# A one-core decoder trunk: how the first arrays are loaded, three filler matmuls, and two places in attention's order

## The chip, the core and the metric

The kernel runs on one core of a Trainium2 chip. The metric is the device time of one execution in microseconds (us); smaller is better. TensorE does the matmuls (PE in the rows, PEld where it loads weights), ScalarE is ACT, VectorE is DVE, GpSimd is POOL, and SyncE is SP, which here only starts transfers. ACT and POOL can start transfers too. A transfer started by any of them is carried out by the core's 16 DMA engines.

## The reference

The input is one sequence of 256 positions with 1024 features in float32. There are two layers. The first is an mLSTM mixer followed by a convolutional feed-forward network; after it, keys and values are computed once from the residual stream. The second is block-sparse attention over those keys and values (with one block of 256 it is plain causal attention), followed by a second feed-forward network. Cut to what matters here:

```
def mlstm_mixer(x, norm_g, w_in, b_gates, h_norm_g, w_out):
    u = rmsnorm(x, norm_g) @ w_in
    q, k, v, o, gi, gf = jnp.split(u, M_SPLITS, axis=-1)
    ...
    h = mlstm_chunkwise(q, k, v, i_pre, f_pre)
    ...
    return h.astype(x.dtype) @ w_out

def shared_kv(x, norm_g, w_kv, k_norm_g, cos, sin):
    kv = rmsnorm(x, norm_g) @ w_kv
    ...

for l in range(DEPTH):
    if l < N_A:
        h = h + mlstm_mixer(...)
    else:
        h = h + moba_mixer(...)
    h = h + conv_ffn(...)
    if l == N_A - 1:
        kb, vb, kmean = shared_kv(h, kv_norm, w_kv, k_norm, cos, sin)
```

## The kernel before

**Tiling.** The residual stream is held transposed in `hT`, eight tiles of 128 features by 256 positions, k = 0 to 7. Every float32 operand is split into a high and a low part in the format float32r, and each product is made of three: high by high, high by low, low by high. ACT makes the high part and DVE the low part (lines 155 to 171). Weights come in units of up to 128 x 2048 elements (1 MB) through three raw buffers and four high/low pairs.

**The start.** Lines 123 to 135 start the first transfers: `hT` in five pieces, the small array `fst` (the gate weights and the first norm's gains, 36 KB), the first weight unit `raw0` in four pieces of 512 columns, and the second unit `raw1` in two. Each column block of 256 in `raw0` belongs to one k. The first two pieces of `raw0` are started by ACT, all else by SP. Every transfer from SP and ACT counts its landing in one of eight semaphores in turn, and waits, before it starts, for the earlier transfer that used the same one.

`warm_up` (lines 146 to 151) gives TensorE ten matmuls on zeros (fillers) while the data come. Then lines 408 to 415 write out by hand, for ACT and DVE, the order in which `hT` is scaled and split into `xa` (which needs `fst`) and `raw0` is split: for k = 0 and 1 each `xa` tile and its weight block, afterwards two `xa` tiles and then a double block of weights. Lines 554 to 557 are the matmuls: for each k two products of two matmuls each (lines 241 and 245) and one for the gates (line 548), k after k; after k = 0 two more fillers stand.

**Attention.** `mix` (line 70) lays small pieces of other work between the matmul steps of a projection; each piece has a due time in estimated us, and it goes in ahead of the first step that begins at or after it. `block_x` is sixteen steps of three matmuls (lines 262 to 264), eight for each half t of the positions; after the eighth step of a half its result goes to `done`. On lines 815 to 828 these pieces are: `r.sums` (the sum of squares over features, line 212, which needs `sqacc` and gives `rc` by way of DVE and POOL; `heads` needs `rc`), `turn` (transposes of query or key heads, line 753, copied out by ACT at line 754), `turn_p` (three transposes of a head's weights, line 781, split by line 168/169 and copied by line 783), `logits` and `values`. `turn` and `turn_p` take their PSUM bank from one set of three (`mis`), so each waits until an earlier one's bank has been read out.

TensorE's order is the program's order everywhere. The order on ACT, DVE and POOL is written by hand up to line 593 for ACT and DVE, and made by the language's scheduler elsewhere.

Of the kernel before, what the change touches and what calls it, by code (L numbers as in the profile page):

```python
# [21 lines left out]
KD = D // P  # L22
# [14 lines left out]
AHEAD = 2  # L37
GROUP = 4
HOLD = 4
WARM = 10  # L40
FILL = 2
WHOLE = 6
PIECES = 2

# [25 lines left out]
def mix(steps, items=()):  # L70

    items, now = list(items), 0.0
    for cost, step in steps:
        while items and items[0][0] <= now:
            items.pop(0)[1]()
        step()
        now += cost
    for _, item in items:
        item()
# [3 lines left out]
def yoco_kernel(ctx: ExitStack, tc: tile.TileContext, A, out):  # L83
    nc = tc.nc
# [30 lines left out]
    hT = keep.tile([P, KD, S], F32, name="hT")  # L115
    fst = const.tile([P, N_FIRST], F32, name="fst")
# [3 lines left out]
    rope = const.tile([P, NT, 2, ROT], F32, name="rope")  # L120
    raw0 = wraw.tile([P, 2048], F32, name="raw")

    nc.sync.dma_start(hT[:, 0], A["xT"][:, 0])
    nc.sync.dma_start(fst, A["first"])
    nc.sync.dma_start(hT[:, 1], A["xT"][:, 1])
    for j in range(3):
        k = slice(2 * j + 2, 2 * j + 4)
        nc.sync.dma_start(hT[:, k], A["xT"][:, k])
    for j in range(4):
        c = slice(j * 512, (j + 1) * 512)  # L130
        (nc.scalar if j < 2 else nc.sync).dma_start(raw0[:, c], A["w_kq"][0, :, c])
    raw1 = wraw.tile([P, 2048], F32, name="raw")
    for j in range(2):
        c = slice(j * 1024, (j + 1) * 1024)
# [11 lines left out]
    def warm_up(n):  # L146
        for j in range(n):
            ps = bank("acc")
            nc.tensor.matmul(ps, warm[:, :P], warm, start=True, stop=True)

    warm_up(WARM)
    nc.vector.memset(wgs.bitcast(F32), 0.0)


    def unit(src, length, pieces=PIECES):
        raw = wraw.tile([P, 2048], F32, name="raw")[:, :length]
        nc.sync.dma_start(raw, src)
        hi = wsp.tile([P, 2048], F32R, name="hi")[:, :length]
        lo = wsp.tile([P, 2048], F32R, name="lo")[:, :length]
        for j in range(pieces):  # L160
            c = slice(j * length // pieces, (j + 1) * length // pieces)
            nc.scalar.activation(hi[:, c], raw[:, c], AF.Copy)  # L162
            nc.vector.tensor_tensor(lo[:, c], raw[:, c], hi[:, c].bitcast(F32), OP.subtract)  # L163
        return hi, lo
# [20 lines left out]
    def operand(pool, name, n):  # L185
        ts = [pool.tile([P, 2 * S], F32R, name=f"{name}{k}") for k in range(n)]
        return [t[:, :S] for t in ts], [t[:, S:] for t in ts], ts

    setA = operand(keep, "xa", KD)
# [63 lines left out]
    def steps_x(t, units, x, done):  # L253

        xh, xl, _ = x
        ts = slice(t * P, (t + 1) * P)
        ps = Once(acc)

        def one(k):
            (hi, lo), p = units[k // 4](), ps()  # L260
            c = slice((k % 4) * 512, (k % 4 + 1) * 512)
            nc.tensor.matmul(p, xh[k][:, ts], hi[:, c], start=k == 0, stop=False)  # L262
            nc.tensor.matmul(p, xh[k][:, ts], lo[:, c], start=False, stop=False)  # L263
            nc.tensor.matmul(p, xl[k][:, ts], hi[:, c], start=False, stop=k == KD - 1)  # L264
            if k == KD - 1:
                done(t, p)

        return [(0.64, lambda k=k: one(k)) for k in range(KD)]

    def block_x(src, first, x, done, u=None):  # L270

        u = u or [Once(lambda j=j: unit(src[first + j], 2048)) for j in range(2)]
        return [s for t in range(NT) for s in steps_x(t, u, x, done)]
# [125 lines left out]
    first = ExitStack()  # L399
# [55 lines left out]
    with tc.tile_pool(name="mls", bufs=1, reuse_waits="tile") as mp, \  # L455
            tc.tile_pool(name="mlw", bufs=2, reuse_waits="tile") as mw, lend("mlp", "mis"):
        r = Rstd()
# [81 lines left out]
        def kq_steps(j):  # L539
            return steps_w(pk[j], wk[j // 2], lambda k: k * 256 + (j % 2) * P, setA, range(KD), KD,  # L540
                           lambda p: whole(p, kq[j]))
# [12 lines left out]
        for k in range(KD):  # L554
            mix((s0[k], s1[k], sg[k]))
            if k == 0:
                warm_up(FILL)
        mix(kq_steps(2)[:1])
# [143 lines left out]
    with tc.tile_pool(name="att", bufs=1, reuse_waits="tile") as mp, \  # L702
            tc.tile_pool(name="atw", bufs=2, reuse_waits="tile") as mw, lend("atl", "mis"), ExitStack() as st:
        r = Rstd()
# [106 lines left out]
        def it(t, fn, *a):  # L811
            return (t, lambda: fn(*a))

        W = A["w_kqv"]
        mix(block_x(W, 0, setA, heads(0, 0)), [it(4.4, r.sums)])
        mix(block_x(W, 2, setA, heads(0, 1)), [it(3.5, turn, 0, 0, 0), it(8.5, turn, 0, 0, 1)])
        mix(block_x(W, 4, setB, heads(1, 0)), [it(3.5, turn, 0, 1, 0), it(8.5, turn, 0, 1, 1), it(9.2, turn, 1, 0, 0)])
        mix(block_x(W, 6, setB, heads(1, 1)),
            [it(4.5, turn, 1, 0, 1)] + [it(6.0 + 1.2 * h, logits, h) for h in range(4)])
        mix(block_x(W, 8, setA, v_done(0)),  # L820
            [it(0.5, turn, 1, 1, 0), it(1.2, turn_p, 0), it(2.6, turn_p, 1), it(4.8, turn_p, 2),
             it(5.2, turn, 1, 1, 1), it(5.8, turn_p, 3)] + [it(6.2 + 1.2 * h, logits, 4 + h) for h in range(4)])
        early.close()
        pp = st.enter_context(tc.tile_pool(name="atp", bufs=1, reuse_waits="tile"))
        pS += [[pp.tile([P, S], F32R, name=f"p{nm}{h}") for nm in "hl"] for h in range(AH // 2, AH)]
# [75 lines left out]
```

## Time and profile before

| what | value |
|---|---|
| median of 3 runs | 594.1 us (593.5 to 594.26) |
| profiled execution, its own time | 594.04 us |
| span of its trace | 592.3 us |
| time outside the span | 1.74 us |
| TensorE busy in the span | 585.9 us (99%) |
| DVE, ACT, POOL busy | 495.0, 394.7, 161.0 us |

The profile is one execution. Its span begins with the first instruction and ends with the last; 594.04 - 592.3 = 1.74 us lie around it. A busy share says how long an engine had an instruction in work, and the chain of waits says what each stretch of time waited for.

### The profile page before, as it was taken

How to read it: one execution, taken by the hardware profiler on the slowest of the kernel's cores; microseconds unless marked ns; L12 is line 12 of the kernel's file. 1: busy time of each engine (PE TensorE's matmuls, PEld its weight loads, DVE VectorE, ACT ScalarE, POOL GpSimd, SP SyncE). 2: the span in 40 equal slices, each digit the busy share in tenths (PEclk: the TensorE clock that was granted, in tenths of full speed). 3: DMA queues.
4: the chain of work that ended last, by engine and by line, in shares of the span. 5: the costliest groups of instructions: out<-in, count | busy, mean ns of one | idle time of the engine just before them, and what ended most of it. 6: DMA issues, size and time to landing. Idle time of an engine off the chain costs nothing.

```text
span 592.3 us, 9008 instructions
## 1 busy us (share of the span) xinstructions
PE 585.9 (99%) x3266; PEld 503.2 (85%) x3266; DVE 495.0 (84%) x843; ACT 394.7 (67%) x731; POOL 161.0 (27%) x178
## 2 busy tenths in 40 slices
PE   8999999999999999999999999999999999999997
PEld 4888888888888888888888878888888888888887
DVE  6888677799999999988867787577999999998750
ACT  6777776487777767765656687646877867675530
POOL 3001300452445443301221210024335543432000
PEclk9999999999999999999999999999999999999999
DMA  8667334347454533487745533343564455345930
GB/s 284 237 222 274 143 142 146 141 152 275 155 188 160 209 132 135 153 266 240 258 167 214 196 127 134 125 139 133 181 237 151 144 211 188 123 148 191 285 116 19
DMA packets 18621, 105.79 MB, mean 179 GB/s; under 512 B 2320, under 2 KB 3856, under 8 KB 9104
## 3 DMA queue, kind: packets, MB, share of 16 engines
q1 hardware_dynamic: 18288, 104.68, 50.4%
q10 hardware_dynamic: 288, 0.52, 0.3%
q8 instruction: 26, 0.43, 0.3%
q14 instruction: 19, 0.16, 0.1%
HBM read 104.15 MB, written 1.05 MB: 178 GB/s over the span
## 4 chain that ended last, share of the span: by engine, by line
PE 97%; DMA 2%; ACT 0%; DVE 0%; issue 0%
PE acc L241 48%; PE acc L245 25%; PE acc L262 6%; PE acc L264 6%; PE acc L263 6%; DMA raw<-w_kq 2%; PE acc L239 1%; PE mis L635 1%; PE mis L753 1%; PE acc L763 1%; PE mis L807 0%; PE mis L781 0%; PE acc L762 0%; PE mis L808 0%; PE mis L667 0%; PE mis L602 0%
## 5 line engine op out<-in xcount | busy, mean ns | idle before, releaser
L163 DVE TENSOR_TENSOR lo<-raw,hi 128x1024 fp32r<-128x1024 f32 (+1 forms) x210 | 238.4, 1166 | 23.2 <-ACT hi L162 23.0
L241 PE MATMUL acc<-xb,hi 128*128 128x512 f32 x736 | 252.1, 396 | 0.0
L162 ACT ACTIVATE hi<-raw 128x1024 fp32r<-128x1024 f32 (+1 forms) x210 | 193.1, 968 | 41.1 <-PE acc L241 14.9
L245 PE MATMUL acc<-xb,lo 128*128 128x256 f32 x736 | 191.2, 279 | 0.0
L241 PEld LDWEIGHTS acc<-xb,hi 128*128 128x128 f32 x736 | 131.8, 188 | 25.1 <-DVE xb L171 0.2
L245 PEld LDWEIGHTS acc<-xb,lo 128*128 128x128 f32 x736 | 138.7, 188 | 8.0
L241 PE MATMUL acc<-f,hi 128*128 128x512 f32 x330 | 115.0, 393 | 0.0
L330 DVE SCALAR_TENSOR_TENSOR y<-whole,par,y 128x255 f32<-128x255 f32 (+1 forms) x176 | 108.1, 635 | 3.7 <-ACT y L327 3.4
L245 PE MATMUL acc<-f,lo 128*128 128x256 f32 x352 | 96.8, 282 | 0.0
L339 POOL TENSOR_TENSOR a<-sg,y 128x256 f32<-128x256 f32 x44 | 54.3, 1235 | 104.3 <-ACT sg L337 104.2
L241 PEld LDWEIGHTS acc<-f,hi 128*128 128x128 f32 x330 | 61.1, 188 | 13.0
L327 ACT ACTIVATE y<-whole,par 128x256 f32<-128x256 f32 x88 | 52.1, 594 | 25.5 <-DVE whole L283 21.9
L245 PEld LDWEIGHTS acc<-f,lo 128*128 128x128 f32 x352 | 66.1, 188 | 1.3
L241 PE MATMUL acc<-xa,hi 128*128 128x512 f32 x160 | 56.4, 396 | 0.4 <-DVE xa L171 0.4
L341 POOL TENSOR_TENSOR f<-a,f 128x256 fp32r<-128x256 f32 x44 | 43.6, 991 | 39.5 <-ACT f L340 39.5
L262 PE MATMUL acc<-hi,xa 128*128 128x512 f32 x128 | 52.6, 411 | 0.0
L264 PE MATMUL acc<-hi,xa 128*128 128x512 f32 x128 | 50.1, 392 | 0.0
L263 PE MATMUL acc<-lo,xa 128*128 128x512 f32 x128 | 50.0, 390 | 0.0
L199 POOL TENSOR_TENSOR sqacc<-sqacc,sq 128x256 f32<-128x256 f32 x18 | 16.1, 892 | 106.3 <-ACT sq L198 106.2
L245 PE MATMUL acc<-xa,lo 128*128 128x256 f32 x160 | 43.5, 285 | 1.2 <-DVE lo L169 1.2
L283 DVE TENSOR_TENSOR whole<-acc,whole 128x256 f32<-128x256 f32 x89 | 36.2, 412 | 0.0
L282 ACT ACTIVATE whole<-acc 128x256 f32<-128x256 f32 x89 | 32.3, 368 | 5.2 <-DVE y L330 5.2
(193 smaller groups left out, 652.5 us busy)
## 6 DMA issues: line engine op xcount, KB each, us to landing
raw<-w_up SPq DMA_DIRECT2D x44, 1024.0 KB, 4.8
raw<-w_down SPq DMA_DIRECT2D x32, 704.0 KB, 5.0
raw<-w_kqv SPq DMA_DIRECT2D x12, 1024.0 KB, 4.9
raw<-w_vo SPq DMA_DIRECT2D x8, 1024.0 KB, 5.1
raw<-w_out SPq DMA_DIRECT2D x4, 1024.0 KB, 4.8
raw<-w_o SPq DMA_DIRECT2D x4, 1024.0 KB, 4.9
raw<-w_kq SPq DMA_DIRECT2D x2, 1024.0 KB, 8.0
raw<-w_kq SPq DMA_DIRECT2D x2, 512.0 KB, 7.5
```

The costliest lines, as they stand in the source:

```text
L162: nc.scalar.activation(hi[:, c], raw[:, c], AF.Copy)
L163: nc.vector.tensor_tensor(lo[:, c], raw[:, c], hi[:, c].bitcast(F32), OP.subtract)
L241: nc.tensor.matmul(p, hi[:, c], both[k], start=k == 0, stop=last)
L245: nc.tensor.matmul(p[:, :S], lo[:, c], xh[k], start=False, stop=False)
L262: nc.tensor.matmul(p, xh[k][:, ts], hi[:, c], start=k == 0, stop=False)
L263: nc.tensor.matmul(p, xh[k][:, ts], lo[:, c], start=False, stop=False)
L264: nc.tensor.matmul(p, xl[k][:, ts], hi[:, c], start=False, stop=k == KD - 1)
L283: nc.vector.tensor_tensor(y, ps[:, :S], y, OP.add)
L327: nc.scalar.activation(y, u, AF.Identity, bias=b, scale=w[2])
L330: nc.vector.scalar_tensor_tensor(y[:, d:], u[:, :S - d], w[j], y[:, d:], op0=OP.mult, op1=OP.add)
L339: nc.gpsimd.tensor_tensor(out=a, in0=sg, in1=y[0], op=OP.mult)
L341: nc.gpsimd.tensor_tensor(out=al[i], in0=a, in1=ah[i].bitcast(F32), op=OP.subtract)
```

## The change

At the start, `fst` is started by POOL and no longer by SP; `hT` comes in four pieces (k = 0, 1, 2 to 3, 4 to 7); `raw0` comes in three pieces (512, 512 and 1024 columns), all started by ACT. The fillers ahead of the first product go from ten to nine, and the two after k = 0 go. In attention `r.sums` stands behind the eighth step of the first half, just ahead of `heads`, where it stood ahead of the eighth step; and `turn(1, 1, 1)` and `turn_p(2)` change places.

```
-WARM = 10
-FILL = 2
+WARM = 9
+FILL = 0
...
+    nc.gpsimd.dma_start(fst, A["first"])
     nc.sync.dma_start(hT[:, 0], A["xT"][:, 0])
-    nc.sync.dma_start(fst, A["first"])
     nc.sync.dma_start(hT[:, 1], A["xT"][:, 1])
-    for j in range(3):
-        k = slice(2 * j + 2, 2 * j + 4)
-        nc.sync.dma_start(hT[:, k], A["xT"][:, k])
-    for j in range(4):
-        c = slice(j * 512, (j + 1) * 512)
-        (nc.scalar if j < 2 else nc.sync).dma_start(raw0[:, c], A["w_kq"][0, :, c])
+    for k0, k1 in ((2, 4), (4, KD)):
+        nc.sync.dma_start(hT[:, k0:k1], A["xT"][:, k0:k1])
+    for k0, k1 in ((0, 2), (2, 4), (4, KD)):
+        c = slice(k0 * 256, k1 * 256)
+        nc.scalar.dma_start(raw0[:, c], A["w_kq"][0, :, c])
...
-        mix(block_x(W, 0, setA, heads(0, 0)), [it(4.4, r.sums)])
+        def first_done(t, ps):
+            if t == 0:
+                r.sums()
+            heads(0, 0)(t, ps)
+
+        mix(block_x(W, 0, setA, first_done))
...
-            [it(0.5, turn, 1, 1, 0), it(1.2, turn_p, 0), it(2.6, turn_p, 1), it(4.8, turn_p, 2),
-             it(5.2, turn, 1, 1, 1), it(5.8, turn_p, 3)] + [it(6.2 + 1.2 * h, logits, 4 + h) for h in range(4)])
+            [it(0.5, turn, 1, 1, 0), it(1.2, turn_p, 0), it(2.6, turn_p, 1), it(4.6, turn, 1, 1, 1),
+             it(5.2, turn_p, 2), it(5.8, turn_p, 3)] + [it(6.2 + 1.2 * h, logits, 4 + h) for h in range(4)])
```

SP's first transfers before (`xT` goes to `hT`; `w_kq` to `raw0` with 512 columns, to `raw1` with 1024, to the third unit with 2048; DMAHW0 to DMAHW7 are the eight semaphores):

```order
L123 DMA hT<-xT 128x256
L124 DMA fst<-first 128x72
L125 DMA hT<-xT 128x256
L128 DMA hT<-xT 128x512 x3
L131 DMA raw<-w_kq 128x512 [waits DMAHW0_49]
L131 DMA raw<-w_kq 128x512 [waits DMAHW1_49]
L135 DMA raw<-w_kq 128x1024 [waits DMAHW2_49]
L135 DMA raw<-w_kq 128x1024 [waits DMAHW3_49]
L157 DMA raw<-w_kq 128x2048 [waits DMAHW4_49]
```

and in the changed kernel:

```order
L124 DMA hT<-xT 128x256
L125 DMA hT<-xT 128x256
L127 DMA hT<-xT 128x512
L127 DMA hT<-xT 128x1024
L134 DMA raw<-w_kq 128x1024
L134 DMA raw<-w_kq 128x1024 [waits DMAHW0_49]
L156 DMA raw<-w_kq 128x2048 [waits DMAHW1_49]
```

`fst` and the second half of `raw0` have left this queue, and the first half of `raw1` no longer waits for a semaphore.

TensorE in attention before, from the last step of the first half on (`pr` is a head's weights in `turn_p`, `y` the queries in `turn`):

```order
L264 MATMUL acc<-hi,xa_132 128x512
L781 MATMUL mis<-ident,pr_3260 128x128 [waits DVE_49,Activation_49]
L781 MATMUL mis<-ident,pr_3260 128x128 [waits DVE_49]
L781 MATMUL mis<-ident,pr_3260 128x128
L262 MATMUL acc<-hi,xa_125 128x512
L263 MATMUL acc<-lo,xa_125 128x512
L264 MATMUL acc<-hi,xa_125 128x512
L753 MATMUL mis<-ident,y_3743 128x128 [waits Activation_49]
```

and in the changed kernel:

```order
L263 MATMUL acc<-hi,xa_128 128x512
L752 MATMUL mis<-ident,y_3735 128x128 [waits DVE_49,Activation_49]
L752 MATMUL mis<-ident,y_3735 128x128 x3
L261 MATMUL acc<-hi,xa_121 128x512
L262 MATMUL acc<-lo,xa_121 128x512
L263 MATMUL acc<-hi,xa_121 128x512
L780 MATMUL mis<-ident,pr_3252 128x128 [waits Activation_49]
```

The query transposes now come first, and the weight transposes stand where the wait for ACT was.

ACT at the same place before (`pr_3258` is the copy that frees the bank of `turn_p(0)`; `vh` is the first half's result):

```order
L170 ACTIVATE vh<-acc,rc 128x512 [waits PE_49]
L168 ACTIVATE xb_139<-mis 128x256 [waits PE_49]
L783 ACTIVATE pr_3258<-mis 128x128 [waits DVE_49]
L783 ACTIVATE pr_3259<-mis 128x128 [waits DVE_49]
L754 ACTIVATE qT<-mis,gcol 128x4x128 [waits PE_49]
```

and in the changed kernel:

```order
L169 ACTIVATE vh<-acc,rc 128x512 [waits PE_49]
L753 ACTIVATE qT<-mis,gcol 128x4x128 [waits PE_49]
L782 ACTIVATE pr_3250<-mis 128x128 [waits DVE_49]
L782 ACTIVATE pr_3251<-mis 128x128 [waits DVE_49]
L167 ACTIVATE xb_135<-mis 128x256 [waits PE_49]
```

Between `vh` and the copy that frees the bank, the query copy of 128 x 512 now stands in place of a split of 128 x 256.

On POOL the transfer of `fst` stands ahead of all the constants, and the clears now come ahead of all the selects and casts, which were mixed before. Elsewhere two neighbours change places on DVE in attention; nothing else moves.

## Rows read from the trace of the kernel before

**Rows 1.** The page: the span, and the busy time of each engine (share of the span, instructions).

```profile
span 592.3 us, 9008 instructions
PE 585.9 (99%) x3266; PEld 503.2 (85%) x3266; DVE 495.0 (84%) x843; ACT 394.7 (67%) x731; POOL 161.0 (27%) x178
```

**Rows 2.** What TensorE waited for in the whole span: total us, times, longest.

```profile
PE acc L149 <- DVE warm L143: 1.2, 1, 1.2
PE acc L245 <- DVE lo L169: 1.2, 2, 1.0
PE acc L241 <- DVE xa L171: 0.4, 1, 0.4
PE mis L753 <- ACT pr L783: 0.2, 1, 0.2
```

**Rows 3.** The chain that ended last, in order of time, its start: start us, us, what.

```profile
0.80 3.36 DMA raw<-w_kq
4.17 6.85 DMA raw<-w_kq
...
12.46 0.38 PE acc L245
```

**Rows 4.** The timeline of the first 20 us: start us, us, engine, line, what it does, and in brackets the idle time before it and what ended that.

```profile
1.25 4.45 PE L149 MATMUL acc<-warm 128*128 128x512 bf16 x10 [1.25 <-DVE warm L143]
4.43 0.51 ACT L170 ACTIVATE xa<-hT,fst 128x256 fp32r<-128x256 f32 x1 [1.22 <-DMA fst<-first]
4.97 0.95 DVE L171 SCALAR_TENSOR_TENSOR xa<-hT,fst,xa 128x256 fp32r<-128x256 f32 x1 [2.70 <-ACT xa L170]
5.70 0.47 POOL L451 CAST amask<-amaskf 128x256 bf16<-128x256 f32 x1
6.07 0.52 PE L241 MATMUL acc<-xa,hi 128*128 128x512 f32 x1 [0.37 <-DVE xa L171]
6.99 0.48 DVE L171 SCALAR_TENSOR_TENSOR xa<-hT,fst,xa 128x256 fp32r<-128x256 f32 x1 [0.40 <-ACT xa L170]
7.17 0.89 ACT L170 ACTIVATE xa<-hT,fst 128x256 fp32r<-128x256 f32 x2
7.33 0.61 PE L149 MATMUL acc<-warm 128*128 128x512 bf16 x2
9.36 0.39 PE L245 MATMUL acc<-xa,lo 128*128 128x256 f32 x1 [0.30 <-DVE lo L169]
10.18 0.40 PE L548 MATMUL acc<-xa,hi 128*128 128x512 f32 x1
11.11 0.40 PE L548 MATMUL acc<-xa,hi 128*128 128x512 f32 x1
```

**Rows 5.** Transfers, asked for one short stretch at a time: those started at 1.23 us (`fst`), 1.70 (k = 1), 3.08 (k = 6 and 7) and 4.17 (the third piece of `raw0`): from and to, queue, KB, us from the start to the landing.

```profile
fst<-first SPq DMA_DIRECT2D x1, 36.0 KB, 3.1
hT<-xT SPq DMA_DIRECT2D x1, 128.0 KB, 4.7
hT<-xT SPq DMA_DIRECT2D x1, 256.0 KB, 5.1
raw<-w_kq SPq DMA_DIRECT2D x1, 256.0 KB, 6.9
```

**Rows 6.** The first 10 us by stretches: busy time of PE, PEld, DVE, ACT, POOL with counts, then the granted clock, the DMA engines' busy share and GB/s.

```profile
0.00:3.00 3.00, 1.75 (x5) 0.64 (x6) 1.18 (x2) 1.28 (x1) 2.35 (x13) 1.00 0.27 82
3.00:6.00 3.00, 2.70 (x7) 0.67 (x5) 1.03 (x2) 1.17 (x4) 3.00 (x16) 1.00 0.94 231
6.00:9.00 3.00, 2.94 (x12) 1.68 (x12) 2.59 (x7) 2.56 (x7) 0.17 (x1) 1.00 0.99 349
9.00:10.00 1.00, 0.70 (x5) 0.59 (x5) 1.00 (x3) 0.38 (x1) 0.00 (x0) 1.00 1.00 332
```

**Rows 7.** The timeline around two places where the sums of line 212 go between two matmuls: the first layer's (24.45 to 25.36 us) and attention's (301.32 to 302.64).

```profile
24.45 0.40 PE L241 MATMUL acc<-xa,hi 128*128 128x512 f32 x1
25.36 0.40 PE L245 MATMUL acc<-xa,lo 128*128 128x256 f32 x2
...
301.32 0.42 DVE L199 TENSOR_TENSOR sqacc<-sqacc,sq 128x256 f32<-128x256 f32 x1
301.46 0.39 PE L264 MATMUL acc<-hi,xa 128*128 128x512 f32 x1
302.64 0.40 PE L263 MATMUL acc<-lo,xa 128*128 128x512 f32 x1
```

**Rows 8.** The timeline of attention's values block: two transposes of queries and two of weights on TensorE, and ACT between them.

```profile
347.84 0.60 PE L753 MATMUL mis<-ident,y 128*128 128x128 f32 x4
348.97 0.49 PE L781 MATMUL mis<-ident,pr 128*128 128x128 f32 x3
353.80 0.49 PE L781 MATMUL mis<-ident,pr 128*128 128x128 f32 x3
354.00 0.69 ACT L170 ACTIVATE vh<-acc,rc 128x512 fp32r<-128x512 f32 x1 [0.44 <-PE acc L264]
354.59 0.37 ACT L168 ACTIVATE xb<-mis 128x256 fp32r<-128x256 f32 x1
354.85 0.47 ACT L783 ACTIVATE pr<-mis 128x128 f32<-128x128 f32 x2
355.18 0.66 PE L753 MATMUL mis<-ident,y 128*128 128x128 f32 x4 [0.19 <-ACT pr L783]
```

## The prediction

> **What bounds the kernel now.** I read the page's head first: TensorE has an instruction in work for 585.9 of 592.3 us [rows 1]. A busy share does not say that TensorE runs without holes, so the second view is what it waited for: five waits in the whole span, four of them in the first 13 us and one of 0.2 us in attention [rows 2]. So the kernel runs at TensorE's pace from about 13 us on, and an edit is worth what it takes out of those few waits or adds to them. The third view is the chain of waits at the start: it is two transfers of the first weight unit, the second started at 4.17 us, until k = 4 begins on TensorE at 12.46 us [rows 3]. The fourth, the timeline, gives the steps: the first product at 6.07 us, k = 2 at 9.36, and 0.93 us for the five matmuls of one k (from 10.18 to 11.11) [rows 4]. After k = 3 TensorE stands still until 12.46.
>
> **The change part by part.** The profiled execution took 594.04 us, its span and 1.74 us around it, and lies 0.06 us under the median of 594.1; the sum is made against 594.04.
>
> *Loads: when k = 4 can begin.* Two things set it in the changed kernel, and the later one counts.
>
> The first is the data. k = 4 now needs all of `hT` (k = 4 to 7 is one piece) and all of `raw0` (its last 1024 columns are one piece), with `fst` 2084 KB, or 2134 thousand bytes. Before, the stretches moved 82, 231 and 349 GB/s for 3 us each, so 246 + 693 + 1047 = 1986 thousand bytes by 9.0 us, and then 332 a us [rows 6]. At that pace the sum is reached at 9.0 + 148/332 = 9.45 us. The stretch from 3 to 6 us was the slow one, and in it lay the small transfers (`fst`, and the 128 KB of k = 1, which took 4.7 us to land) [rows 5]. Nine transfers of SP and ACT led up to the third piece of `raw0`; now seven of them bring everything, and `fst` goes by POOL. Had that stretch run at 349 GB/s, 354 thousand bytes would have come earlier, 1.0 us, and the data be there at 8.4. I take 9.1, somewhat nearer to the measured pace. From the first `xa` of a pair to TensorE's start on that pair were 9.36 - 7.17 = 2.19 us [rows 4]; before, the `xa` of k = 4 and 5 were made ahead of the late weights, now they come with them, so all 2.19 us count. k = 4 begins at 9.1 + 2.19 = 11.3 us; between 10.6 and 11.65 for the two ends.
>
> The second is the chain of splits. It begins when `fst` lands: ACT's first `xa` waited for it until 4.43 us, and k = 2 began 4.93 us later [rows 4]. In that chain DVE stood 0.40 us, because k = 1 came late; its transfer now starts one place earlier, so 4.53 us remain. With two k of 0.93 us, k = 4 cannot begin before the landing of `fst` plus 6.5 us. No row shows a transfer of POOL. From below I take the 3.1 us that `fst` needed on SP, from 0.80 us: 3.9. From above the slowest of the first transfers, 4.7 us: 5.5 [rows 5]. That gives 10.4 to 12.0 us. I take a landing at 4.3, since 3.1 us is the row of the same array, and so 10.8, under the 11.3 of the data.
>
> So k = 4 goes from 12.46 to 11.3: **-1.16 us**. It stays gained, because TensorE waits nowhere for the next 300 us [rows 2]; k = 6 and 7 followed k = 4 and 5 without one before [rows 2], and `raw1` is started earlier than before. On ACT a third start stands ahead of the table load; ACT waited 1.22 us ahead of its first `xa` [rows 4], which covers it. On SP the later loads stand two places earlier. On POOL the constants wait for the start of `fst`; none is needed before TensorE's sums at about 24.5 us [rows 7], but for one clear that ACT's table warm-up reads, and ACT has those 1.22 us.
>
> *Fillers.* Ten took 4.45 us, 0.445 each [rows 4]. One fewer ends the row at 5.25 us, under the first product in any of these cases; the two behind k = 0 ran at 7.33 us, while k = 1 waited for DVE. Nothing gained, nothing lost.
>
> *The sums in attention.* From the matmul ahead of them to the second behind it the sums took 25.36 - 24.45 = 0.91 us in the first layer and 302.64 - 301.46 = 1.18 in attention [rows 7]. The 0.27 us are a wait for the last addition to `sqacc`, which runs from 301.32 for 0.42 us. One step later, 0.68 us, it is done: **-0.27 us**. `rc` comes 0.41 us later, and with it `heads` on ACT; TensorE is then in the second half, in another bank.
>
> *The two transposes.* A query transpose takes TensorE 1.13 us to the next such piece, a step of matmuls included (347.84 to 348.97), and the weight transposes are one transpose of 0.11 shorter, 1.02 [rows 8]. Before, 355.18 - 353.80 = 1.38 lay between them, a wait of 0.36 us for ACT's copy, which began at 354.85 and freed the bank 0.33 us later. Now the queries come at 353.80 without a wait and the weight transposes are due at 354.93, but they need that same bank. On ACT the copy now stands behind the query copy, which follows `vh` and is as large: it starts at 354.59, lasts 0.59 until the next, so the bank is free at 354.59 + 0.59 + 0.33 = 355.51 [rows 8]. The wait is 0.58 us: **+0.22 us**, between -0.36 (no wait) and that.
>
> The sum: 594.04 - 1.16 - 0.27 + 0.22 = 592.83, so **592.8 us**. A measurement of this kernel tells differences from about 0.2% on, 1.19 us; faster by that begins at 592.9.
>
> **The rivals.**
>
> *A, the start runs through.* The data are there by 8.4 us and `fst` by 3.9: k = 4 begins at 10.6, and TensorE does k = 1 to 7 with hardly a hole. 594.04 - 1.86 - 0.05 = **592.1 us**. For it: seven transfers in place of nine. Against it: 349 GB/s was never held before 6 us [rows 6].
>
> *B, POOL and DVE meet.* DVE's first split took 0.95 us while POOL was at its constants, until 6.17, and 0.48 us afterwards [rows 4]. POOL's selects and casts now come later and in one row, so they can meet four or five of the splits, not one or two. Two more doubled ones, 1.0 us, put k = 4 at 10.8 + 1.0 = 11.8; with a landing of `fst` at 4.7 it is 12.2. 594.04 - 0.26 to 0.66 - 0.05 = **593.5 us**. The Trainium skill, SBUF — State Buffer, "Who interferes with whom", says that a DVE instruction with two inputs in SBUF contends with a POOL instruction that reads SBUF, and not with one that only writes it. By that rule the move of the selects behind the clears is the harmful part of POOL's new order; the 0.95 beside 0.48 agrees.
>
> *C, slower: the second weight unit overtakes.* `raw1`'s first half waited for a semaphore before; now it is started right behind `hT`, without a wait, while ACT's queue still holds the last 512 KB of `raw0`. If the DMA engines serve it first, k = 4 needs 512 KB more, 524 thousand bytes at 332 a us, and the data are there at 9.45 + 1.6 = 11.0 us; k = 4 begins at 13.2: 594.04 + 0.75 - 0.05 = **594.7 us**. It costs from a landing at 12.46 - 2.19 = 10.3 on. The third piece before landed late in just this manner, 6.9 us after its start, where the pieces of `hT` ahead of it took 5.1 [rows 5]. Against it: two queues that share evenly end together.
>
> *D, the lower clock lasts.* The granted clock reads 1.00 throughout [rows 6], but a filler of 512 columns each 0.445 us is the pace of 1.2 GHz, and 2048 columns of one k in 0.93 us that of 2.4. With fewer fillers the step up may come later. Should k = 0 to 3 run at 1.2 GHz, they take 1.7 us each from about 5.9 on, and k = 4 begins at 12.7: **594.2 us**.
>
> **How the numbers follow.** The forecast has 0.53 (592.3 to 593.3 by itself), A 0.15, B 0.17, C 0.11, D 0.04. Faster by over 0.2%: half and a little of the forecast, 0.30, and A, 0.45. Slower by over 0.2%, over 595.3: the far end of C, 0.05. Within: 0.50. The range from 592.0 to 594.6 leaves out the ends of A and C, under two in ten.
>
> **What would show it.** In the changed profile: `fst` lands near 4.3 us; both 512 KB pieces land near 9.1, within half a us of each other; TensorE starts k = 4 near 11.3, behind a wait for DVE; the sums of attention take 0.9 us with no wait on `sqacc`; the wait for ACT's copy now stands ahead of the weight transposes of line 780, about 0.6 us. The forecast is wrong if the large pieces land after 10.3, if DVE's splits of k = 1 to 3 take twice 0.48, or if waits turn up after 13 us where there were none.

## The result, and the profile after

The changed kernel takes 597.23 us (median of 6 runs, 596.54 to 597.69), beside 593.25 us (592.82 to 594.26) for the kernel before in the same comparison: a ratio of 1.0063, 95% interval 1.0052 to 1.0073. It is slower by 4.0 us, and the time lies outside the predicted range. The profiled execution took 597.15 us: a span of 595.4 and 1.75 around it. Line numbers of the changed kernel are one lower than before up to the attention block.

The page's head and what TensorE waited for in the whole span (total us, times, longest), to be read beside [rows 1, 2]:

```profile
span 595.4 us, 9000 instructions
PE 585.5 (98%) x3263; PEld 505.0 (85%) x3263; DVE 494.6 (83%) x843; ACT 394.7 (66%) x731; POOL 161.6 (27%) x179
```

```profile
PE acc L240 <- DVE xa L170: 4.8, 1, 4.8
PE acc L148 <- DVE warm L142: 1.2, 1, 1.2
PE mis L780 <- ACT pr L782: 0.4, 1, 0.4
```

The wait ahead of k = 4 is gone, but one wait of 4.8 us stands ahead of the first product, where there were 0.4. The chain that ended last, its start (start us, us, what; beside [rows 3]), tells what it is for:

```profile
0.69 0.62 issue
1.31 7.07 DMA fst<-first
8.40 0.52 ACT xa L169
8.94 0.50 DVE xa L170
9.57 0.76 PE acc L240
```

`fst`, started by POOL at 1.31 us, lands at 8.38. The first product begins at 9.57, where it began at 6.07 [rows 4]. The other transfers of the start, by the time from issue to landing (beside [rows 5]; each asked for by its issue):

```profile
hT<-xT SPq DMA_DIRECT2D x1, 128.0 KB, 5.7
raw<-w_kq ACTq DMA_DIRECT2D x1, 512.0 KB, 8.7
hT<-xT SPq DMA_DIRECT2D x1, 256.0 KB, 8.4
hT<-xT SPq DMA_DIRECT2D x1, 512.0 KB, 9.3
```

These are k = 1, the last piece of `raw0`, k = 2 and 3, and k = 4 to 7. They are late too: k = 1 took 4.7 us before, a piece of 256 KB of `hT` about 5 [rows 5]. The stretches of the start (busy time of PE, PEld, DVE, ACT, POOL; granted clock; the DMA engines' busy share; GB/s; beside [rows 6]):

```profile
3.00:6.00 3.00, 1.79 (x6) 0.49 (x4) 0.00 (x0) 0.69 (x2) 2.96 (x15) 1.00 0.94 173
6.00:9.00 3.00, 0.00 (x0) 0.00 (x0) 0.06 (x1) 0.60 (x2) 1.28 (x7) 0.76 0.94 353
9.00:10.00 1.00, 0.43 (x1) 0.46 (x2) 1.00 (x4) 1.00 (x4) 0.00 (x0) 0.50 1.03 369
12.00:14.00 2.00, 2.00 (x8) 1.66 (x7) 2.00 (x5) 2.00 (x6) 0.00 (x0) 0.50 1.05 442
16.00:20.00 4.00, 4.00 (x23) 3.44 (x22) 2.92 (x6) 2.27 (x8) 0.00 (x0) 1.00 0.94 356
```

From 3 to 6 us the DMA engines moved 173 GB/s, where they moved 231. And TensorE, which stood from 4.8 us on, reads a granted clock of 0.50 in the stretches from 9 to 14 us, the level of 1.2 GHz. The timeline shows the price by the gate matmul that ends each k (k = 0, 1, 2 and 3):

```profile
10.99 0.63 PE L547 MATMUL acc<-xa,hi 128*128 128x512 f32 x1
12.69 0.63 PE L547 MATMUL acc<-xa,hi 128*128 128x512 f32 x1
14.40 0.41 PE L547 MATMUL acc<-xa,hi 128*128 128x512 f32 x1
15.34 0.40 PE L547 MATMUL acc<-xa,hi 128*128 128x512 f32 x1
```

One k takes 1.70 us at the lower clock and 0.94 at the higher one. At that pace the late pieces of `hT` and `raw0` are there before TensorE asks for them, so that their lateness shows in no wait.

In attention both edits did what was worked out. The sums follow without a wait, 306.03 - 305.11 = 0.92 us where there were 1.18 [rows 7], and the weight transposes now wait for ACT, 358.22 - 356.53 = 1.69 us after the query transposes:

```profile
305.11 0.39 PE L263 MATMUL acc<-hi,xa 128*128 128x512 f32 x1
305.34 0.50 PE L211 MATMUL mis<-tri,sqacc 128*128 128x1 f32 x4
...
306.03 0.40 PE L262 MATMUL acc<-lo,xa 128*128 128x512 f32 x1
...
356.53 0.60 PE L752 MATMUL mis<-ident,y 128*128 128x128 f32 x4
...
358.22 0.55 PE L780 MATMUL mis<-ident,pr 128*128 128x128 f32 x3 [0.39 <-ACT pr L782]
```

### The profile page after: what moved, and what is told of

It reads as the page before. It is cut to its first block, busy times and chain, and to the rows that moved or that the text cites. A ratio compares the mean times of both kernels' runs of the same rounds, so it can differ in the third digit from the quotient of the medians.

```text
span 595.4 us, 9000 instructions
## 1 busy us (share of the span) xinstructions
PE 585.5 (98%) x3263; PEld 505.0 (85%) x3263; DVE 494.6 (83%) x843; ACT 394.7 (66%) x731; POOL 161.6 (27%) x179
## 3 DMA queue, kind: packets, MB, share of 16 engines
q1 hardware_dynamic: 17712, 104.12, 49.6%
## 4 chain that ended last, share of the span: by engine, by line
PE 98%; DMA 1%; ACT 0%; issue 0%; DVE 0%; POOLq 0%
PE acc L240 48%; PE acc L244 25%; PE acc L261 6%; PE acc L263 6%; PE acc L262 6%; DMA fst<-first 1%; PE acc L238 1%; PE mis L634 1%; PE acc L762 1%; PE mis L752 1%; PE mis L780 0%; PE mis L806 0%; PE acc L547 0%; PE mis L807 0%; PE acc L761 0%; PE mis L666 0%
## 5 line engine op out<-in xcount | busy, mean ns | idle before, releaser
L240 PE MATMUL acc<-xa,hi 128*128 128x512 f32 x160 | 57.9, 405 | 4.8 <-DVE xa L170 4.8
L240 PEld LDWEIGHTS acc<-xa,hi 128*128 128x128 f32 x160 | 30.1, 193 | 11.1 <-ACT hi L167 5.2
```

What stands on the lines that cost most here:

```text
L240: nc.tensor.matmul(p, hi[:, c], both[k], start=k == 0, stop=last)
```

## The experiments

The theories at the outset: T1, POOL's late landing is the whole loss. T2, the regrouped loads cost as well. T3, the idle stretch of TensorE lets the clock fall, which is paid on top. Later ones are named where they come up: R, ACT's third piece of the first weight unit takes the DMA engines from `hT`; G, larger pieces of `hT` cost; F, missing fillers cost. The median of the kernel before was between 593.18 and 593.34 us in each comparison.

**e1: the small array back on SP.**

```
-    nc.gpsimd.dma_start(fst, A["first"])
     nc.sync.dma_start(hT[:, 0], A["xT"][:, 0])
+    nc.sync.dma_start(fst, A["first"])
```

> The changed kernel, with only the small array back on SP's queue, second as before. Kernel before 593.25 us, changed kernel 597.23. Theory T1 (POOL's late landing of the small array is the whole loss, the rest of the change does what the prediction said): k = 4 near 11.3 us on TensorE, time 592.0 to 592.4. Theory T2 (the larger pieces cost too, whoever loads the small array): the piece of hT for k = 2 and 3 lands near 10 and the one for k = 4 to 7 near 11.5, as they did in the changed kernel, so k = 2 begins near 12.3 and k = 4 near 13.7, time 593.25 + 1.2 - 0.05 = 594.4, and more if the granted clock falls. If neither, and the loss was elsewhere: still near 597.

596.9 us, ratio 1.0059 (1.0043 to 1.0075). T1 falls: without POOL the kernel is as slow. `fst` lands 3.5 us after its start and the first product begins at 6.05 as before, but k = 1 of `hT` takes 5.9 us and k = 1 begins on TensorE only at 9.04, so that TensorE waits twice for the low parts:

```profile
PE acc L244 <- DVE lo L168: 1.9, 2, 1.6
PE acc L148 <- DVE warm L142: 1.2, 1, 1.2
PE acc L240 <- DVE xa L170: 0.9, 1, 0.9
```

The clock fell back here too: it reads 0.50 in the stretches from 9 to 14 us of the profiled run. The two of its six runs whose mean granted clock is 1.000 took 595.8 and 595.9 us, the four with 0.993 to 0.994 took 596.5 to 598.5. So with `fst` on SP the loads still cost, and the clock costs too where it falls; e9 takes the two apart. A mean of 1.000 says only that no fall is on record: before its first step up the clock reads 1.00 as well, as in [rows 6] from 0 to 3 us, where a filler took 0.445 us, the pace of 1.2 GHz [rows 4].

**e2: only the small array by POOL.**

```
+    nc.gpsimd.dma_start(fst, A["first"])
     nc.sync.dma_start(hT[:, 0], A["xT"][:, 0])
-    nc.sync.dma_start(fst, A["first"])
```

> The kernel before, with only the small array moved to POOL's queue, first of all transfers. T1: it lands near 8.4 us as in the changed kernel, the first product begins near 9.5, TensorE stands from 5.7 on, the granted clock falls: 593.25 + 3 to 4 = 596 to 597.5. If the late landing came from the new company on the queues (T2 alone), it lands by 5.5, the first product is at 6.7 at the latest and the time stays within 0.6 us of 593.25. If the landing is late and the clock does not matter (not T3): about 593.25 + 1.5 = 594.8, since the chain of splits then puts k = 4 at 8.4 + 6.5 = 14.9 less what the late weights let it catch up.

596.31 us, ratio 1.0047 (1.0032 to 1.0062). `fst` needs 5.8 us from its issue at 1.31, and TensorE waits 3.1 us ahead of the first product:

```profile
fst<-first POOLq DMA_DIRECT2D x1, 36.0 KB, 5.8
```

So POOL's transfer is late in the old company as well, and moving `fst` costs 3.0 us by itself. In the profiled run that includes a stretch at the lower clock, which reads 0.50 from 9 to 10 us.

**e3: attention alone.**

```
-        mix(block_x(W, 0, setA, heads(0, 0)), [it(4.4, r.sums)])
+        mix(block_x(W, 0, setA, first_done))
...
-it(4.8, turn_p, 2), it(5.2, turn, 1, 1, 1)
+it(4.6, turn, 1, 1, 1), it(5.2, turn_p, 2)
```

> The kernel before, with only the two reorderings in attention. Sum of the prediction: -0.27 + 0.22 = -0.05 us, so 593.2 and no difference that can be measured (all theories of the start agree); the sums of attention follow without a wait on sqacc, and the wait for ACT's copy ahead of the weight transposes is 0.5 to 0.6 us in place of 0.2 to 0.36. If more than 0.5 us either way, the attention part has a cost that the prediction did not see.

593.09 us, ratio 0.9996 (0.9988 to 1.0005): no difference, as worked out.

**e4: fillers until the small array is there.**

```
-WARM = 9
+WARM = 28
```

> The changed kernel with 28 fillers in place of nine ahead of the first product, so that TensorE has work until about 9 to 10 us, when the small array has landed by POOL. T3 (the idle stretch lets the granted clock fall to half, and that is paid on top of the late landing): the granted clock reads 1.00 throughout, each k takes 0.93 us in place of 1.28, and the time falls from 597.23 to where the late data put it: k = 2 near 12.3, k = 4 near 13.7, so 594.4 to 595.0. If the clock costs nothing beside the landing (not T3): the time stays at 597, or a little above for fillers that end after the small array is there.

595.6 us, ratio 1.0037 (1.0024 to 1.005), 1.6 us under the changed kernel but above the 594.4 to 595.0 that were expected, and the granted clock reads 1.00 throughout:

```profile
3.00:6.00 3.00, 3.00 (x13) 1.27 (x12) 0.00 (x0) 0.68 (x2) 2.96 (x15) 1.00 0.92 118
6.00:9.00 3.00, 2.78 (x13) 1.08 (x11) 0.00 (x0) 0.33 (x1) 1.28 (x7) 1.00 0.96 323
9.00:10.00 1.00, 0.16 (x1) 0.19 (x1) 0.79 (x3) 1.00 (x5) 0.00 (x0) 1.00 1.04 424
12.00:14.00 2.00, 1.43 (x8) 1.14 (x8) 2.00 (x5) 2.00 (x6) 0.00 (x0) 1.00 1.06 438
```

T3 holds: 19 matmuls on zeros more make the kernel faster, though the first product begins no sooner (9.84 us). It stays slower than the kernel before, so the late data cost too.

**e5: the last piece of the unit by SP.** The changed kernel as in e1, and

```
-        nc.scalar.dma_start(raw0[:, c], A["w_kq"][0, :, c])
+        (nc.scalar if k0 < 4 else nc.sync).dma_start(raw0[:, c], A["w_kq"][0, :, c])
```

> The changed kernel with the small array back on SP's queue, and the last 512 KB of the first weight unit started by SP behind hT in place of ACT (one 1024-column piece still, so hT in four and the unit in three). With ACT starting that piece and SP the small array, 596.9 us. Theory R (ACT's third piece takes the DMA engines from hT: two queues share by packets, and ACT's are 2048 and 4096 bytes where SP's are 1024 and 2048): k = 1 of hT lands near 6.0 again in place of 7.6, its matmuls begin near 7.9, all of hT is there near 8.4 and the last weights near 9.6, k = 4 begins near 11.8: 593.3 - 0.7 = 592.6. Theory G (the grouping of hT in larger pieces delays it): k = 2 and 4 late as before, 595 to 596. Theory F (the fillers that are gone let the clock fall): granted clock at half in part of the first 15 us, 594 to 595.5.

594.5 us (592.97 to 595.96), ratio 1.0019 (1.001 to 1.0029), 2.4 under e1 by that one edit. R's direction holds, its number was missed by 1.9. F's 594 to 595.5 holds the time too; e11 shows what the fillers are worth with these loads.

**e6: the unit alone.** The kernel before with `raw0` in three pieces, all by ACT (the two lines of the change's diff).

> The kernel before with one part of the change alone: the first weight unit in three pieces (512, 512, 1024 columns), all started by ACT. R: hT's k = 1 lands near 7.5 us in place of 5.9 and the rest of hT one to two us later too, k = 1 and 2 begin late, 593.3 + 2.5 to 3.5 = 596 to 597. G and F: 593.3 or, since the weights come earlier, down to 592.5.

595.21 us, ratio 1.0036 (1.0023 to 1.0049). k = 1 of `hT` and `fst` took longer (4.7 and 3.1 in [rows 5]):

```profile
hT<-xT SPq DMA_DIRECT2D x1, 128.0 KB, 6.2
fst<-first SPq DMA_DIRECT2D x1, 36.0 KB, 5.0
```

R's direction holds, at 1.9 us in place of 2.5 to 3.5. The clock may have a part in this: it reads 0.50 from 9 to 10 us of the profiled run. But two of the four runs have no fall on record (a mean of 1.000), and they took 595.1 us too.

**e7: the pieces of `hT` alone.** The kernel before with `hT` in four pieces.

> The kernel before with one part of the change alone: hT in four pieces (k = 0, 1, 2 to 3, 4 to 7) in place of five. R and F: the bytes of hT come at the same pace and the weights of k = 4 and 5 still behind them, one semaphore sooner: 593.3, at most 0.5 either way. G: k = 4 waits for all of the last piece and k = 2 for its company: 594.5 to 596.

593.1 us (592.75 to 595.74), ratio 1.0003 (0.9992 to 1.0013). G falls: this part costs nothing that can be told.

**e8: the fillers alone.**

```
-WARM = 10
-FILL = 2
+WARM = 9
+FILL = 0
```

> The kernel before with one part of the change alone: nine fillers in place of ten and none behind k = 0. The prediction's term is 0, so 593.3. F: TensorE stands 0.45 us longer ahead of the first product and 0.6 us behind k = 0, and in part of the runs the granted clock falls to half for some us: 594 to 595.5. R and G: 593.3.

595.1 us (593.56 to 595.68), ratio 1.0026 (1.0014 to 1.0037): the edits that the prediction put at nothing cost 1.8 us. Of the five runs, however, only one has a mean granted clock under 0.999, the profiled one. There the clock reads 0.50 from 9 to 10 us, and k = 4 began at 12.12 us, 0.5 to 0.8 us later than in the seven traces named in the next section. The rest of its loss lies near 50 us: a weight transfer that landed late at 49.6 us, and a wait behind it:

```profile
49.65 2.01 ACT L162 ACTIVATE hi<-raw 128x1024 fp32r<-128x1024 f32 x2 [3.10 <-DMA raw<-w_vo]
53.32 0.70 PE L602 MATMUL mis<-kq,kq 128*128 128x256 f32 x2 [0.82 <-DVE E L528]
```

So F is only partly borne out here (more in e13 and e14).

**e9: the loads alone, TensorE kept busy.** The changed kernel as in e1, and

```
-WARM = 9
-FILL = 0
+WARM = 14
+FILL = 8
```

> The changed kernel with the small array back on SP's queue, as in the first experiment (596.9 us), and now 14 fillers ahead of the first product and eight behind k = 0, so that TensorE does not stand idle before 9 us. What is left over the kernel before (593.3) is then the loads alone, less 0.2 for attention. Theory R (ACT's third piece takes the DMA engines from hT and delays it): k = 1 of hT still lands past 7, k = 4 near 12.7 to 13.5, 594.3 to 595.3. If the fillers (that is, the clock) were the whole of that loss: 593.5 or less. The granted clock should show no half after the step up, by either.

594.73 us (594.3 to 595.04), ratio 1.002 (1.0011 to 1.0029), clock without a fall. Against e1 the fillers give back 2.2 us; 1.5 us remain for the loads. k = 4 began at 12.96. The eight fillers behind k = 0 are not what holds it: they kept k = 1 until 9.21 us, where its splits were done at 8.69, but k = 2 still had to wait for its own:

```profile
11.00 0.39 PE L244 MATMUL acc<-xa,lo 128*128 128x256 f32 x1 [0.51 <-DVE lo L168]
```

**e10: four fillers more in the kernel before.**

```
-WARM = 10
+WARM = 14
```

> The kernel before with four fillers more ahead of the first product (14 in place of 10), nothing else. With one fewer and none behind k = 0 it took 595.1 in place of 593.3. If what counts is that TensorE has work until the first product is ready, 593.3 falls by 0 to 0.6 us (592.7 to 593.3), since in most runs the small array lands later than in the profiled run. If the fillers ahead are enough as they are and it was the two behind k = 0 that counted: 593.3 to 593.9, since four fillers at 0.2 to 0.4 us end past the time at which the first product could begin.

593.16 us, ratio 0.9994 (0.9985 to 1.0003): no difference; the ten were enough.

**e11: the parts that cost nothing, together.** e5's loads and attention with 14 and two fillers.

> The parts that cost nothing, together: the kernel before with hT in four pieces, the first weight unit in three of which ACT starts two and SP the last behind hT, the two reorderings in attention, 14 fillers ahead of the first product and two behind k = 0, and the small array on SP's queue. If the loss of the same loads with nine and no fillers (594.5) was the fillers': k = 4 near 11.7 as in that kernel's trace, no half clock, 592.3 to 592.9. If the 1024-column piece itself costs: 594 or more.

593.36 us, ratio 1.0001 (0.9993 to 1.001), 0.5 above what was expected: 1.1 under e5, which has the same loads with nine and no fillers, but no gain over the kernel before. The last piece of `raw0` landed at 10.9 us, and k = 4 began at 12.33. Beside e9, from which it differs in who starts that piece (and in six fillers behind k = 0), it is 1.4 us faster. In e9, k = 1 and the pieces of `hT` behind it took

```profile
hT<-xT SPq DMA_DIRECT2D x1, 128.0 KB, 5.6
hT<-xT SPq DMA_DIRECT2D x1, 256.0 KB, 6.6
hT<-xT SPq DMA_DIRECT2D x1, 512.0 KB, 7.4
```

and in e11

```profile
hT<-xT SPq DMA_DIRECT2D x1, 128.0 KB, 4.9
hT<-xT SPq DMA_DIRECT2D x1, 256.0 KB, 5.0
hT<-xT SPq DMA_DIRECT2D x1, 512.0 KB, 5.8
```

The queues' own rows for the first 8 us (packets, MB, share of the 16 engines; q10 carries ACT's transfers, q1 SP's) say why, first e9:

```profile
q10 hardware_dynamic: 432, 1.05, 40.3%
q1 hardware_dynamic: 576, 0.62, 24.8%
```

and then e11:

```profile
q1 hardware_dynamic: 740, 1.18, 43.4%
q10 hardware_dynamic: 288, 0.52, 25.6%
```

Together they moved 1.7 MB by 8 us in both; what ACT's queue moved more in e9, SP's queue moved less. The last pieces changed places too: `raw0` was complete at 8.1 us in e9 and 10.9 in e11, `hT` at 10.0 and 8.5. This is R, seen in the transfers themselves.

**e12: POOL and SP in a quiet stretch.** Two spare loads of the small array in attention:

```
+        for probe, queue in ((fq, nc.gpsimd), (fs, nc.sync)):
+            nc.scalar.activation(probe[:, :NT], r.rc, AF.Copy)
+            queue.dma_start(probe, A["first"])
```

> The kernel before plus two copies of the small array's load into spare tiles, one started by POOL and one by SP, in attention near 305 us, where the DMA engines are nearly idle (two small copies on ACT make them wait until there). P1, POOL's start is late by itself: its landing comes 4 to 6 us after the issue also there, SP's near 2. P2, only the crowd on the engines at the start makes it late: both land within 2 to 3 us. The time of the kernel tells nothing here.

```profile
fs<-first SPq DMA_DIRECT2D x1, 36.0 KB, 1.8
fq<-first POOLq DMA_DIRECT2D x1, 36.0 KB, 2.3
```

P1 falls. POOL's way is half a us longer than SP's here, and not 3.

**e13 and e14: the two filler edits apart.** `WARM = 9` alone, and `FILL = 0` alone.

> The kernel before with nine fillers ahead of the first product in place of ten, the two behind k = 0 kept. If the idle time ahead of the first product is what costs (the clock falls back some us after the fillers end): about 595 like both edits together. If it is the pair behind k = 0: 593.3. If the loss of both together was mostly a late weight transfer near 48 us that came up in those runs by chance: 593.3 here and in the other one.

> The kernel before without the two fillers behind k = 0, ten ahead kept. If the pair behind k = 0 is what costs: about 595. If the idle time ahead of the first product is: 593.0 to 593.3, since TensorE then only waits 0.3 us longer for DVE behind k = 0.

e13 593.6 us (592.78 to 595.55), ratio 1.0006 (0.9997 to 1.0016); e14 593.11, ratio 0.9999 (0.999 to 1.0008). Neither alone is told from nothing, though e13 spreads further up than the kernel before (to 594.25 in that comparison). That both together cost 1.8 us, in five runs, is not explained by these.

**e15: two more probes of POOL.** One in the quiet stretch with four multiplications behind it on POOL (two of them at once, two after another operation), one later.

> The kernel before plus two more loads of the small array into spare tiles, both started by POOL in attention: one near 304 us, where the DMA engines are idle, with two multiplications of 128 x 256 (1 us each) right behind it on POOL; one near 313 us, where SP's loads of 1 MB keep the engines busy, with little behind it on POOL. In the quiet stretch with nothing behind it, it landed after 2.3 us. If POOL's own following work makes the start late: the first lands after 3.5 us or more, the second near 2.5 to 3. If the crowd does: the first near 2.3, the second after 4 us or more. The time of the kernel tells nothing here.

```profile
fa<-first POOLq DMA_DIRECT2D x1, 36.0 KB, 2.4
fb<-first POOLq DMA_DIRECT2D x1, 36.0 KB, 2.2
```

POOL's own following work does not make it late. The second probe was issued only at 319.25 us, after the crowd that it was meant for, so it tells nothing of that.

**e16: smaller packets on ACT's queue.** e9, and

```
-    for k0, k1 in ((0, 2), (2, 4), (4, KD)):
-        c = slice(k0 * 256, k1 * 256)
+    for j in range(4):
+        c = slice(j * 512, (j + 1) * 512)
         nc.scalar.dma_start(raw0[:, c], A["w_kq"][0, :, c])
```

> The changed kernel with the small array on SP, 14 fillers ahead and eight behind k = 0 (594.7 us), and now the first weight unit in four pieces of 512 columns, still all started by ACT: the last 512 KB go in packets of 2048 bytes in place of 4096, the same bytes on the same queue. If the size of the packets decides how two queues share: hT's pieces for k = 1 and for k = 2 and 3 land near 6.5 and 8 us in place of 7.3 and 8.8, 593.6 to 594.2. If it is that ACT's queue carries all 1 MB at all: 594.7.

594.37 us (594.01 to 594.79), ratio 1.0018 (1.0009 to 1.0026), 0.36 under e9, of the 1.5 us at stake. k = 1 of `hT` took 5.3 us, k = 2 and 3 6.6. The piece of k = 2 and 3 thus came no sooner than in e9 (6.6). The size of the rows is not all that changed: the unit takes four transfers in place of three, and the last piece of `hT` started at 4.15 us in place of 2.64. So the part of the packets' size stays open; with small ones, too, most of the loss remains while ACT's queue carries the whole megabyte.

**e17: a probe of POOL among other transfers.**

> The kernel before plus one more load of the small array into a spare tile, started by POOL in attention near 315 us, while SP's loads of 1 MB move some 400 GB/s (an addition of 128 x 4 on POOL makes it wait until there). In quiet stretches it landed 2.2 to 2.4 us after its issue. If busy DMA engines make POOL's transfers late: 3.5 us or more. If not, 2.2 to 3, and what makes it 5.8 to 7.3 at the start is something that only the start has. The time of the kernel tells nothing here.

```profile
fb<-first POOLq DMA_DIRECT2D x1, 36.0 KB, 2.2
```

It was issued at 315.93 us, while SP's loads moved 418 to 434 GB/s (windows of 1 us until 317), and its first packet came 1.48 us later, just behind them. One full queue does not hold up POOL's first packet; what POOL's packets would do among others was not seen.

**e18: the weights of k = 4 and 5 ahead of the last piece of `hT`.** The kernel before, with the sums moved, `WARM = 12`, and on SP:

```
     nc.sync.dma_start(hT[:, 1], A["xT"][:, 1])
+    for j in range(4):
+        if j > 0:
+            k = slice(2 * j, 2 * j + 2)
+            nc.sync.dma_start(hT[:, k], A["xT"][:, k])
+        if j > 1:
+            c = slice(j * 512, (j + 1) * 512)
+            nc.sync.dma_start(raw0[:, c], A["w_kq"][0, :, c])
```

> The kernel before with the weights of k = 4 and 5 started by SP ahead of the last piece of hT (so that k = 4 needs 256 KB less ahead of it), the sums of attention behind their eighth step, and 12 fillers ahead. By the bytes: 262 thousand at 332 a us are 0.8 us, so k = 4 begins near 10.8 in place of 11.4 to 11.6, no wait behind it; with the sums' 0.27: 593.25 - 0.6 to 0.8 - 0.27 = 592.2 to 592.5. If the chain of splits on ACT and DVE sets k = 4 instead (the landing of the small array plus 6.5): 592.9 to 593.2.

592.89 us (592.55 to 593.18), ratio 0.9991 (0.9982 to 1.0): the lowest of all, at the edge of what can be told. Its trace has one wait of 0.3 us between the first product and 350 us, and k = 4 begins at 11.36 straight behind k = 3. Now the chain of splits sets the start, the second case of the expectation: `fst` landed at 4.68 us, k = 1 began at 7.88, k = 2 at 9.38 behind that wait, much as in [rows 4], and TensorE's own pace counts only from there on.

## Why the prediction was wrong

The loss adds up along a row of kernels: the kernel before 593.25; the new loads and attention, with `fst` on SP and TensorE kept busy (e9), 594.7, that is +1.5; `fst` by POOL, TensorE still kept busy, with 28 and no fillers in place of 14 and eight (e4), 595.6, that is +0.9; the few fillers (the changed kernel), 597.2, that is +1.6. The shares depend on the order: with few fillers, `fst` by POOL adds only 0.3 us (e1 to the changed kernel), and the fillers are worth 2.2 (e1 to e9).

*What bounds the kernel* was read rightly as to the place, but from one execution. That execution took 594.04 us, 0.8 over the median measured later, and its k = 4 began at 12.46 us [rows 3]. In seven later traces of kernels with the same loads (e3, e10, e12 to e15, e17) it began between 11.29 and 11.63. One of them, e13:

```profile
10.83 0.40 PE L241 MATMUL acc<-xa,hi 128*128 128x512 f32 x1
11.06 0.40 PE L548 MATMUL acc<-xa,hi 128*128 128x512 f32 x1
11.29 0.28 PE L245 MATMUL acc<-xa,lo 128*128 128x256 f32 x1
```

Here k = 4 follows k = 3 without a gap, and the third piece of `raw0` landed 4.9 us after its start, not 6.9 [rows 5]. So the 11.3 us that were to be won are where the kernel mostly stood already; the wait ahead of k = 4 is one that these executions don't have (e17 has one of 0.8 us ahead of k = 6 in its place).

*Loads, the data.* This step failed. The landing of the large pieces was put at 9.1 us, between 8.4 and 9.45, by a sum of bytes at the old pace; they landed at 10.4 (`raw0`) and 11.5 (`hT`). The prediction's own sign for this was a landing after 10.3. The pace is the smaller part of this. The changed kernel moved 89, 173 and 353 GB/s for 3 us each and then 369, so as many bytes as k = 4 needs had moved by 9.8 us. But the sum treated all bytes as one stream: bytes of later transfers, `raw1`'s first of all, must be among them. The prediction's own rows could have shown that. By its sum the 1872 thousand bytes up to the third piece of `raw0` had moved by 8.7 us, and that piece landed at 11.0 [rows 3].

The sum was also made for k = 4 alone. In e1, e4, e6, e9 and e16, where ACT carries the whole unit, `hT`'s piece with k = 2 and 3 landed between 8.7 and 10.5 us (at 7.1 in the kernel before), and k = 2 began 2.22 to 2.24 us behind it, close to the prediction's 2.19. For that piece the prediction has no term. In e9 it set the pace: k = 4 followed k = 3 without a wait at 12.96, though its own data had been there since 10.0. And k = 1, which was to come earlier because it starts one place earlier, started at 1.23 us in place of 1.70 and landed at 6.9 in place of 6.4.

In the runs, ACT's queue with the whole unit on it drew the DMA engines away from `hT`, on which the first matmuls wait (e6, e9 against e11). The stretch from 3 to 6 us did not become faster: 173 GB/s. How much of that is the loads' is not shown, since it moved 209 in e9 with the same pieces, and 207 to 231 in the traces with the loads of before. The Trainium skill, DMA: Bandwidth & Descriptors, "Issuing engines are not separate DMA queues", says that starting transfers on several engines only saves the time to start them. The measurement differs: the same piece on ACT's or SP's queue is 1.4 us of the kernel (e9 and e11). The same page, "Queues, rings and completion order", says that a DMA engine goes round the queues packet by packet. e16 agrees in sign, by 0.36 us, but is no clean test of it.

*Loads, `fst`.* This step failed too: its landing was taken at 4.3 us, at most 5.5, and measured 8.38 here, 7.07 in e2. It was started at 1.31 us, not at 0.80, and took 7.1 us and 5.8. The upper bound was a row of SP's queue, and no row of POOL's was there to be had. Why POOL's transfer is so late at the start stays open.

*Fillers.* The third failure, as large as the loads'. They were put at zero because they end before the first product in any case. That holds, and it was the wrong question: with nine of them and a first product at 9.57 us TensorE stands for 4.8 us, and the clock goes back to 0.50. More fillers are worth 1.6 us with `fst` by POOL (597.2 to 595.6), 2.2 with it on SP (596.9 to 594.7) and 1.1 with e5's loads (594.5 to 593.4). With the old loads they are worth nothing above ten (e10), and what is lost below that is not settled: 1.8 us in e8, 0.4 in e13 and within its interval, none in e14. Whether e8's excess is the clock, the late transfer at 49.6 us, or chance in five runs, stays open. That the fillers act through the clock is shown in the profiled executions, by one k in 1.70 us in place of 0.94. The longest runs of e5 and e8 (595.96 and 595.68 us) have no fall on record (0.999 and 1.000), and what made them long was not seen.

*Attention.* Right in both terms, -0.26 and a wait moved and grown by 0.2 (0.39 in the waits); that the sum is near nothing agrees with e3, which can't tell 0.05 us.

*The rivals.* A did not come. B was not put to the test: POOL was done at 7.3 us and DVE's splits began at 8.9, at 0.48 us each. C did not come as it was told: the first half of `raw1` landed at 12.8 us, behind both large pieces. That some of its bytes went ahead of theirs follows from the sum above; what this cost was not tested. D was the nearest, at a chance of 0.04: the clock is one of the large terms, but in the profiled executions by a fall after idle time and not by a late rise. In the others a late rise can't be told, since the clock reads 1.00 before it too.

## What to carry to other kernels

A wait in one profiled execution is a candidate, not a gain: look at it in several executions, above all where it ends with a transfer. Try a sum of bytes on a landing that is already in the rows before it is used for a new one. Before a transfer is moved to another queue, ask which earlier-needed data share the DMA engines with it, since the sum does not tell who is served first; and give a first use of a queue that no row shows a far wider upper bound, or measure it. Fillers are not free to leave out when the data may come later than the fillers last: price the matmuls behind the idle stretch at the lower clock too.

## What was not expected of the hardware

POOL's transfer of 36 KB landed 2.2 to 2.4 us after its issue in attention and 5.8, 7.1 and 7.3 at the start (e2, the changed kernel, e4); its first packet came 1.3 to 1.5 us after the issue in attention, and 3.5 to 5.0 at the start. The Trainium skill, DMA: Bandwidth & Descriptors, "Latency and other measured facts", gives about 1 us to the first byte for transfers by GpSimd; attention is near it, the start is not. In attention neither POOL's own next work (e15) nor one full queue of SP (e17) made it late; two full queues of small packets, DVE's clear of 128 x 1024 next to it, and whatever else only the start has were not told apart.

In e1 the clock fell back though no wait there was longer than 1.6 us: TensorE had waited 0.9 us, done five matmuls, and waited again. In e9, with 14 and eight fillers, it did not fall. A wait of 1.8 us ahead of the first product went without a fall in the profiled run of e5, and one of 1.9 with a fall in that of e8.
